# State space mixer of a two-layer backbone: running sums of log decays spread over partitions by way of DRAM, decayed products into one bank

## The chip, the core and the metric

The kernel runs on one core of a Trainium2 chip. The metric is the time of one execution on the device in microseconds (us). The engines are named as in the profile: PE (TensorE; PEld are its weight loads), DVE (VectorE), ACT (ScalarE), POOL (GpSimd) and SP (SyncE, which issues most DMAs). All arithmetic is float32; GEMM operands are split into a high and a low part of type fp32r.

## What is computed

Two layers of a hybrid block on 256 latent and 256 context tokens: an input projection feeds a bidirectional state space mixer (16 heads of 64, 4 groups with 128 states, chunks of 128 tokens) and a differential attention; both are gated, merged and followed by a gated MLP with a convolution. The change lies in the mixer alone. For each direction (the backward one on flipped tokens) the reference computes

```python
a = (dt * a_head)...; a_cs = jnp.cumsum(a, axis=-1)
cb = jnp.einsum('bclgn,bcsgn->bgcls', cc, bc)
decay_in = jnp.exp(segsum(a))            # exp(a_cs[l] - a_cs[s]) for s <= l, else 0
y_diag = jnp.einsum('bgcls,bgrcls,bcsgrp->bclgrp', cb, decay_in, xd)
...
y_off = jnp.einsum('bclgn,bcgrpn,bgrcl->bclgrp', cc, h_in, jnp.exp(a_cs))
y = (y_diag + y_off).reshape(bsz, n, n_heads, p)
```

## The kernel before

Channels lie on partitions, tokens on the free axis. In layer 0 four blocks t of 128 tokens are worked on (0 and 1 latent, 2 and 3 context, N = 512), in layer 1 the outputs of the two latent blocks alone (N = 256). Every GEMM goes through `gemm_f` (lines 379 to 413): SP loads weight tiles of 128x4x256 into `raw` (line 305, three buffers), ACT casts them to `whi` (line 314), DVE subtracts for `wlo` (line 315), and PE runs three matmuls per block of 128 rows (lines 408 to 410 where 512 columns are taken, 394 to 396 otherwise).

Beside the GEMMs run two lanes of generators. `pump()` (line 341) is called every six GEMM matmuls of 512 columns, or every twelve of 256, and moves each lane by one `yield`. So the program order of everything else follows the GEMM, and matmuls made by `pmm` keep that order on PE. The scheduler orders the other engines ahead of time; on the chip each engine takes its instructions in the fixed order.

In the state space stage the GEMMs are the projections of the inner channels (`xs`), of two pairs of gates and of `z`. Lane 0 runs `states(g)` for the four groups (lines 896 to 937): it transposes `xs` and B, weighs `xs` on POOL (line 920) and carries the states `h`. Lane 1 runs `outputs(g)` (lines 939 to 1010). Per group and block t it does:

- `head(t)`: the product `cb` of B and C, masked for both directions into `cbm` (line 950); then four products `at` on POOL (line 955), a triangular mask times the high and low part (`aH`, `aL`) of the log decays of four heads, for each direction;
- `seg`: four matmuls of 512 columns with a strict triangle `sgt` (line 970), which make the differences of running sums for both directions in one bank, and their Exp to `E` on ACT (line 972);
- X: for each head `cbm` times the step sizes of both directions (ACT line 976, DVE line 977), times E (line 978);
- `yoff`: C times the incoming state of each direction (line 988), each times `ecs`, the Exp of the running sums (DVE line 991, from PSUM), added up if there are two (line 995);
- `yd`: four products of `xT` and X with 64 columns of weights each (line 1000), then `yt` added to the same banks by a product with the identity (line 1003).

Blocks 0 and 1 have an incoming state from both directions, blocks 2 and 3 from one. At the end of a group `xs` takes `yd` and the skip term (line 1007), and the `z` GEMM's part waits for groups that are done (line 1033). The running sums and step sizes are made earlier, between the attention heads and the B projection (lines 817 to 858).

The profile names the PSUM banks by tag and use: `pmmmm` and `psmm` are GEMM banks, `psseg`, `psyoff`, `pscb`, `psstate`, `psssT` the banks of the lanes, `pyyd` the output bank. Lines of `pmm` and `ptr` are shown as L85 and L88.

## Time and profile before

| | |
|---|---|
| median of 3 runs | 1767.27 us (1766.97 to 1767.33) |
| the profiled execution, its own time | 1765.24 us |
| its span, first to last instruction | 1763.5 us |
| granted TensorE clock, mean | 0.995 |
| busy: PE, PEld, DVE, ACT, POOL | 96%, 81%, 66%, 47%, 12% |

"Busy" is the share of the span in which an engine had an instruction running. PE's matmuls are pipelined, so a PE that is busy need not be at its peak. Times inside the run count from the first instruction. In a list of groups the number behind the bar is the idle time ahead of the group's instructions and what ended it. Rows quoted from the trace stand in a section of their own below.

### The profile page before, as it was taken

The page shows a single profiled execution, that of the slowest core. Times are in us where ns is not written, and L with a number is a line of the kernel's source. Part 1 is how long each engine was busy: PE and PEld are TensorE (multiplying, and loading weights), DVE is VectorE, ACT ScalarE, POOL GpSimd, SP SyncE. Part 2 cuts the span into 40 slices and gives each one's busy share as a digit, 9 for nine tenths or more (in the row PEclk, how much of TensorE's full clock was granted, in tenths as well). Part 3 has the DMA queues.
Part 4 walks back from the last instruction along what each step waited for, and adds up shares of the span by engine and source line. Part 5 has one row for each costly group of instructions (what it writes and reads, how often), then busy time and mean ns, then how long its engine had stood idle before and what let it go on. Part 6 is the DMA issues. An engine that isn't in the chain of part 4 may idle for free. (4 is left out here: it accounts for less than half of the span.)

```text
span 1763.5 us, 26823 instructions
## 1 busy us (share of the span) xinstructions
PE 1697.9 (96%) x10483; PEld 1431.3 (81%) x10483; DVE 1159.8 (66%) x2017; ACT 830.3 (47%) x1545; POOL 220.0 (12%) x244
## 2 busy tenths in 40 slices
PE   6999999999998999999999999999999998989997
PEld 4788878777776788888888889788889787989997
DVE  4676677335679865666666326666675788769964
ACT  3565575323333433644444225556554443556653
POOL 3000000003356300300000002100001244010000
PEclk9999999999999999999999999999999999989999
DMA  9643433543220134232233335845435232556653
GB/s 316 205 134 120 128 113 110 178 156 121 59 72 26 51 103 139 89 94 89 93 95 93 96 105 159 251 145 155 146 94 177 75 90 78 179 168 186 187 180 118
DMA packets 226159, 227.98 MB, mean 129 GB/s; under 512 B 10269, under 2 KB 222656, under 8 KB 226032
## 3 DMA queue, kind: packets, MB, share of 16 engines
q1 hardware_dynamic: 224192, 224.56, 41.6%
...
HBM read 222.04 MB, written 4.19 MB: 128 GB/s over the span
## 5 line engine op out<-in xcount | busy, mean ns | idle before, releaser
L315 DVE TENSOR_TENSOR wlo<-raw,whi 128x1024 fp32r<-128x1024 f32 (+1 forms) x318 | 390.5, 1228 | 264.1 <-ACT whi L314 263.4
L314 ACT CAST whi<-raw 128x1024 fp32r<-128x1024 f32 (+1 forms) x318 | 329.4, 1036 | 400.2 <-PE pmmmm L409 164.3
L408 PE MATMUL pmmmm<-th,whi 128*128 128x512 f32 x744 | 307.2, 413 | 0.4 <-DVE chv L573 0.4
L409 PE MATMUL pmmmm<-tl,whi 128*128 128x512 f32 x744 | 295.6, 397 | 0.0
L410 PE MATMUL pmmmm<-th,wlo 128*128 128x512 f32 x744 | 295.0, 396 | 0.0
L408 PEld LDWEIGHTS pmmmm<-th,whi 128*128 128x128 f32 x744 | 140.0, 188 | 39.7 <-issue 7.5
L410 PEld LDWEIGHTS pmmmm<-th,wlo 128*128 128x128 f32 x744 | 139.8, 188 | 33.7 <-issue 1.0
L409 PEld LDWEIGHTS pmmmm<-tl,whi 128*128 128x128 f32 x744 | 140.2, 188 | 29.8 <-issue 1.4
L394 PE MATMUL pmmmm<-th,whi 128*128 128x256 f32 x480 | 139.2, 290 | 0.2 <-ACT th L543 0.2
L396 PE MATMUL pmmmm<-th,wlo 128*128 128x256 f32 x480 | 135.8, 283 | 0.8 <-DVE wlo L315 0.8
L395 PE MATMUL pmmmm<-tl,whi 128*128 128x256 f32 x480 | 135.5, 282 | 0.0
L394 PEld LDWEIGHTS pmmmm<-th,whi 128*128 128x128 f32 x480 | 91.3, 190 | 4.8 <-issue 3.6
L522 POOL TENSOR_TENSOR rs<-ms,mhalf 128x2 f32<-128x2 f32 x9 | 6.3, 699 | 692.3 <-DVE ms L519 692.3
L396 PEld LDWEIGHTS pmmmm<-th,wlo 128*128 128x128 f32 x480 | 91.1, 190 | 1.5 <-DVE wlo L315 1.4
L395 PEld LDWEIGHTS pmmmm<-tl,whi 128*128 128x128 f32 x480 | 91.4, 190 | 0.8 <-issue 0.4
L955 POOL TENSOR_TENSOR at<-kt,aH 128x512 fp32r<-128x512 f32 x48 | 58.0, 1208 | 182.0 <-PE pmmmm L410 100.5
L410 PE MATMUL psmm<-th,wlo 128*128 128x512 f32 x200 | 79.4, 397 | 0.0
L408 PE MATMUL psmm<-th,whi 128*128 128x512 f32 x200 | 79.1, 396 | 0.0
L409 PE MATMUL psmm<-tl,whi 128*128 128x512 f32 x200 | 79.1, 395 | 0.0
L728 ACT ACTIVATE e<-psscore,nmx 128x512 f32<-128x512 f32 (+1 forms) x96 | 58.1, 610 | 42.8 <-DVE nmx L725 39.9
L442 PE MATMUL pmmmm<-whi,th 128*128 128x256 f32 x256 | 74.4, 290 | 0.0
L725 DVE TENSOR_REDUCE nmx<-psscore 128x1 f32<-128x512 f32 (+1 forms) x80 | 51.9, 685 | 33.9 <-PE psscore L85 33.6
...
## 6 DMA issues: line engine op xcount, KB each, us to landing
raw<-in_w_in_dram SPq DMA_DIRECT2D x124, 512.0 KB, 4.0
raw<-in_w_up_dram SPq DMA_DIRECT2D x88, 512.0 KB, 3.5
mraw<-in_w_mod_dram SPq DMA_DIRECT2D x80, 512.0 KB, 4.6
raw<-in_w_down_dram SPq DMA_DIRECT2D x45, 512.0 KB, 3.6
boot<-in_w_mod_dram SPq DMA_DIRECT2D x16, 512.0 KB, 9.4
raw<-in_w_br_att_dram SPq DMA_DIRECT2D x16, 512.0 KB, 3.5
raw<-in_w_br_ssd_dram SPq DMA_DIRECT2D x16, 512.0 KB, 3.6
raw<-in_w_out_dram SPq DMA_DIRECT2D x16, 512.0 KB, 3.6
```

The costliest lines, as they stand in the source:

```text
L314: pin(A.copy(hi[:, 0:n, :], raw[:, 0:n, :]))
L315: pin(V.tensor_tensor(lo[:, 0:n, :], raw[:, 0:n, :], hi[:, 0:n, :].bitcast(F32), op=ALU.subtract))
L394: T.matmul(o[f], whi[:, kk, cs], xh, start=first, stop=False)
L395: T.matmul(o[f], whi[:, kk, cs], xl, start=False, stop=False)
L396: T.matmul(o[f], wlo[:, kk, cs], xh, start=False, stop=last)
L408: T.matmul(o, whi[:, k % 4, cs], hi[k][:, 0:n], start=k == 0, stop=False)
L409: T.matmul(o, whi[:, k % 4, cs], lo[k][:, 0:n], start=False, stop=False)
L410: T.matmul(o, wlo[:, k % 4, cs], hi[k][:, 0:n], start=False, stop=k == k_tiles - 1)
L442: T.matmul(b[:, n, :], hi[k][:, ts], whi[:, k % 4, :], start=k == 0 and n == 0, stop=False)
L725: V.tensor_reduce(nmx[:, cc, 0:ng], sc[cc].rearrange("p (g k) -> p g k", g=ng), axis=AX.X, op=ALU.max, negate=True)
L728: A.activation(e[cc][:, g * w:(g + 1) * w], sc[cc][:, g * w:(g + 1) * w], AF.Exp, bias=nmx[:, cc, g:g + 1], accum_out=sm[:, cc, g:g + 1])
L955: G.tensor_tensor(at, tri[dr].unsqueeze(1).to_broadcast([P, 4, P]), part.bitcast(F32)[:, t, 16 * dr + 4 * g:16 * dr + 4 * g + 4].unsqueeze ...
```

## The change

The differences of running sums are no longer made by matmuls. Once per layer, with the step sizes, four matmuls with the log decays as weights and both triangles as moving operand give the running sums with heads on partitions (`p3`); ACT copies them out, and POOL writes them to DRAM (`csd`) in 8 DMAs. `csc` keeps the running sums with tokens on partitions, as before, but without the Exp. For each block SP fetches four heads of both directions back as `cs`, each row repeated on all 128 partitions (0.5 MB, two buffers). From `cs` come

- `cc`: Exp of `cs` on ACT for the directions that the block has, times C on DVE, 128x1024 elements or 128x512;
- `E`: `cs` less `csc` on POOL, one subtraction of 128x512 per direction, in place; the minimum of both directions on DVE; Exp on ACT. The minimum picks the direction that the mask of `cbm` keeps.

The states then multiply `cc` straight into `yd`: per direction four products with 64 columns of weights each. `seg`, `yoff`, `yt` and the identity product are gone, and with them `sgt`, `aH`, `aL` and `ecs`. The fetch of block t+2 is issued behind X of block t; a block now takes three yields instead of six.

```diff
@@ -655,9 +653,8 @@
         BF = [mp.tile([P, 512], F32, name=f"BF{i}_{j}") for j in range(4)]
         CF = [mp.tile([P, N], F32, name=f"CF{i}_{j}") for j in range(4)]
         dtT = mp.tile([P, 4, 64], F32, name=f"dtT{i}")
-        aH = mp.tile([P, 4, 32], F32R, name=f"aH{i}")
-        aL = mp.tile([P, 4, 32], F32R, name=f"aL{i}")
-        ecs = mp.tile([P, 4, 32], F32, name=f"ecs{i}")
+        csc = mp.tile([P, 4, 32], F32, name=f"csc{i}")
+        csd = dp.tile([4, 2, 16, P], F32, name=f"csd{i}")
         ddt = mp.tile([P, 4, 32], F32, name=f"ddt{i}")
         etot = mp.tile([P, 4, 32], F32, name=f"etot{i}")
 
@@ -843,8 +840,6 @@
             V.scalar_tensor_tensor(dtT[:, :, 0:32], u, 0.0, lw, op0=ALU.max, op1=ALU.add)
             V.tensor_tensor(dtT[:, :, 32:64], dtT[:, :, 0:32], L["A"].unsqueeze(1).to_broadcast([P, 4, 32]), op=ALU.mult)
             av = dtT[:, :, 32:64]
-            V.tensor_copy(aH, av)
-            V.tensor_tensor(aL, av, aH.bitcast(F32), op=ALU.subtract)
             p1, p2 = bank("s"), bank("s")
             for n, lhs in enumerate((tri[0], tri[1], strict[0], strict[1])):
                 T.matmul(p1[:, n * P:(n + 1) * P], lhs, av, start=True, stop=True)
@@ -852,8 +847,18 @@
             p1v = p1.rearrange("p (n t c) -> p n t c", n=4, t=4)
             for dr in range(2):
                 cs = slice(16 * dr, 16 * dr + 16)
-                A.activation(ecs[:, :, cs], p1v[:, dr, :, cs], AF.Exp)
+                V.tensor_copy(csc[:, :, cs], p1v[:, dr, :, cs])
                 A.activation(ddt[:, :, cs], p1v[:, 2 + dr, :, cs], AF.Exp)
+
+            p3 = bank("s")
+            for t in range(4):
+                T.matmul(p3[32 * t:32 * t + 32, 0:256], av[:, t, :], kt[:, C_LE:C_LE + 256], start=True, stop=True)
+            csr = lp.tile([P, 256], F32, tag="h", name=nm("csr"), bufs=4)
+            A.copy(csr, p3[:, 0:256])
+            for t in range(4):
+                for dr in range(2):
+                    r = 32 * t + 16 * dr
+                    G.dma_start(csd[t, dr], csr[r:r + 16, dr * P:(dr + 1) * P])
             A.activation(etot, p2[:, 0:P].rearrange("p (t c) -> p t c", t=4), AF.Exp)
             V.tensor_tensor(ddt, ddt, dtT[:, :, 0:32], op=ALU.mult)
 
@@ -942,34 +947,44 @@
             xT, h_in = sh["xT"], sh["h"]
             yb = [bank("y", "yd"), bank("y", "yd")]
 
-            def head(t):
+            def fetch(t):
+                cs = up.tile([P, 2, 4, P], F32, tag="cs", name=nm("cs"), bufs=2)
+                nc.sync.dma_start(cs.rearrange("p d h l -> p d (h l)"),
+                                  csd[t, :, 4 * g:4 * g + 4, :].rearrange("d h l -> d (h l)").partition_broadcast(P))
+                return cs
+
+            def head(t, cs):
                 tsl = slice(t * P, (t + 1) * P)
                 cb = bank("s", "cb")
                 pmm(cb[:, 0:P], BF[g][:, tsl], CF[g][:, tsl], start=True, stop=True)
                 cbm = up.tile([P, 2, P], F32, tag="cbm", name=nm("cbm"), bufs=2)
                 V.tensor_tensor(cbm, cb[:, 0:P].unsqueeze(1).to_broadcast([P, 2, P]), tri2, op=ALU.mult)
-                ats = []
+
+                cc = up.tile([P, 2, 4, P], F32, tag="cc", name=nm("cc"), bufs=2)
+                dirs = [dr for dr in range(2) if not (dr == 0 and t == 2) and not (dr == 1 and t == 3)]
+                d0, d1 = dirs[0], dirs[-1] + 1
+                A.activation(cc[:, d0:d1], cs[:, d0:d1], AF.Exp)
+
                 for dr in range(2):
-                    for part in (aH, aL):
-                        at = up.tile([P, 4, P], F32R, tag="at", name=nm("at"), bufs=4)
-                        G.tensor_tensor(at, tri[dr].unsqueeze(1).to_broadcast([P, 4, P]),
-                                        part.bitcast(F32)[:, t, 16 * dr + 4 * g:16 * dr + 4 * g + 4].unsqueeze(2).to_broadcast([P, 4, P]),
-                                        op=ALU.mult)
-                        ats.append((dr, at))
-                return cbm, ats
-
-            nxt = head(0)
+                    G.tensor_tensor(cs[:, dr], cs[:, dr],
+                                    csc[:, t, 16 * dr + 4 * g:16 * dr + 4 * g + 4].unsqueeze(2).to_broadcast([P, 4, P]),
+                                    op=ALU.subtract)
+                V.tensor_tensor(cs[:, 0], cs[:, 0], cs[:, 1], op=ALU.min)
+                E = cs[:, 1]
+                A.activation(E, cs[:, 0], AF.Exp)
+                V.tensor_tensor(cc[:, d0:d1].rearrange("p d h l -> p (d h) l"), cc[:, d0:d1].rearrange("p d h l -> p (d h) l"),
+                                CF[g][:, tsl].unsqueeze(1).to_broadcast([P, 4 * (d1 - d0), P]), op=ALU.mult)
+                return cbm, cc, E, dirs
+
+            raw = fetch(0)
+            yield 1
+            nxt = head(0, raw)
+            if NT > 1:
+                raw = fetch(1)
             yield 1
             for t in range(NT):
                 tsl = slice(t * P, (t + 1) * P)
-                cbm, ats = nxt
-                yield 1
-
-                sg = bank("s", "seg")
-                for n, (dr, at) in enumerate(ats):
-                    pmm(sg, sgt[:, dr, :], at.rearrange("p h l -> p (h l)"), start=n == 0, stop=n == 3)
-                E = up.tile([P, 4, P], F32, tag="E", name=nm("E"), bufs=1)
-                A.activation(E, sg.rearrange("p (h l) -> p h l", h=4), AF.Exp)
+                cbm, cc, E, dirs = nxt
                 X = up.tile([P, 4, P], F32, tag="X", name=nm("X"), bufs=2)
                 for h in range(4):
                     dcol = [dtT[:, t, 16 * dr + 4 * g + h:16 * dr + 4 * g + h + 1] for dr in range(2)]
@@ -978,29 +993,21 @@
                 V.tensor_tensor(X, X, E, op=ALU.mult)
                 yield 1
                 if t + 1 < NT:
-                    nxt = head(t + 1)
+                    nxt = head(t + 1, raw)
                     yield 1
+                if t + 2 < NT:
+                    raw = fetch(t + 2)
                 while "done" not in sh:
                     yield None
-                dirs = [dr for dr in range(2) if (dr, t) in h_in]
-                yo = bank("s", "yoff")
-                for dr in dirs:
-                    pmm(yo[:, dr * 256:(dr + 1) * 256], CF[g][:, tsl], h_in[dr, t], start=True, stop=True)
-                yt = up.tile([P, 2, 4, 64], F32, tag="yt", name=nm("yt"), bufs=2)
-                for dr in dirs:
-                    V.tensor_tensor(yt[:, dr], yo[:, dr * 256:(dr + 1) * 256].rearrange("p (h q) -> p h q", h=4),
-                                    ecs[:, t, 16 * dr + 4 * g:16 * dr + 4 * g + 4].unsqueeze(2).to_broadcast([P, 4, 64]),
-                                    op=ALU.mult)
-                if len(dirs) == 2:
-                    V.tensor_tensor(yt[:, 0], yt[:, 0], yt[:, 1], op=ALU.add)
-                yield 1
-                ytv = yt[:, dirs[0]].rearrange("p h q -> p (h q)")
-                for h in range(4):
-                    r = slice(64 * (h % 2), 64 * (h % 2) + 64)
-                    pmm(yb[h // 2][r, tsl], xT[:, t, h * 64:(h + 1) * 64], X[:, h, :], start=True, stop=False)
-                yield 1
                 for f in range(2):
-                    pmm(yb[f][:, tsl], ytv[:, f * P:(f + 1) * P], ident, start=False, stop=True)
+                    for h in (2 * f, 2 * f + 1):
+                        r = slice(64 * (h % 2), 64 * (h % 2) + 64)
+                        pmm(yb[f][r, tsl], xT[:, t, h * 64:(h + 1) * 64], X[:, h, :], start=True, stop=False)
+                    for dr in dirs:
+                        for h in (2 * f, 2 * f + 1):
+                            r = slice(64 * (h % 2), 64 * (h % 2) + 64)
+                            pmm(yb[f][r, tsl], h_in[dr, t][:, h * 64:(h + 1) * 64], cc[:, dr, h, :],
+                                start=False, stop=dr == dirs[-1])
                 yield 1
             for f in range(2):
                 j = 2 * g + f
```

Left out of the diff: `sgt` and the copy into it. Behind the change all lines are a few higher: line 978 is 993 there, 930 is 935, 950 is 961, 315 is 314, 1007 is 1014; the fetch is 952, the subtraction 969, the minimum 972, the product for `cc` 975.

What the change does to the order on PE, seen where a block with one direction is finished in layer 0. Before, from the last `seg` matmul of the block to the product with the identity:

```order
2240 L85 MATMUL psseg_5256<-at_5244,sgt 128x512
2241 L85 MATMUL psyoff_5273<-h_4679,CF_2_621 128x256
2242 L85 MATMUL pscb_5301<-CF_3_622,BF_3_618 128x128
2243 L408 MATMUL pmmmm_5292<-th_253,whi_4872 128x512
2244 L409 MATMUL pmmmm_5292<-tl_254,whi_4872 128x512
2245 L410 MATMUL pmmmm_5292<-th_253,wlo_4873 128x512
2246 L408 MATMUL pmmmm_5292<-th_255,whi_5090 128x512
2247 L409 MATMUL pmmmm_5292<-tl_256,whi_5090 128x512
2248 L85 MATMUL pyyd_4998<-X_5263,xT_4604 64x128 x2
2249 L85 MATMUL pyyd_4999<-X_5263,xT_4604 64x128 x2
2250 L85 MATMUL pyyd_4998<-kt,yt_5275 128x128
2251 L85 MATMUL pyyd_4999<-kt,yt_5275 128x128
```

And now such a block (the same block t = 3 of the same group):

```order
2125 L407 MATMUL pmmmm_5039<-th_260,whi_5029 128x512
2126 L85 MATMUL pyyd_4788<-X_5067,xT_4566 64x128 x2
2127 L85 MATMUL pyyd_4788<-cc_5010,h_4643 64x128 x2
2128 L85 MATMUL pyyd_4789<-X_5067,xT_4566 64x128 x2
2129 L85 MATMUL pyyd_4789<-cc_5010,h_4643 64x128 x2
2130 L408 MATMUL pmmmm_5039<-tl_261,whi_5029 128x512
2131 L409 MATMUL pmmmm_5039<-th_260,wlo_5030 128x512
2132 L85 MATMUL psstate_5099<-xd_5083,bT_4939 128x256
```

All of a block's products now stand in one run between GEMM matmuls, and nothing of it is left ahead of them but `cb`. Behind the stage's first transposition 418 GEMM matmuls stood ahead of the last write into `yd` in layer 0, now 389; in layer 1 454, now 446.

On DVE in layer 0, before, from the product with E of one block into the work on its `yt`:

```order
593 L978 TENSOR_TENSOR X_5046<-X_5046,E_5044 128x512
594 L950 TENSOR_TENSOR cbm_5068<-pscb_5066,kt 128x256
595 L315 TENSOR_TENSOR wlo_5097<-raw_5088,whi_5096 128x1024
596 L1032 SCALAR_TENSOR_TENSOR zt_5078<-zt_5078,pmmmm_4984 128x512
597 L977 SCALAR_TENSOR_TENSOR X_5163<-cbm_5068,dtT_623,X_5163 128x128
598 L1034 TENSOR_TENSOR xs_3_3867<-xs_3_3867,zt_5078 128x512
599 L991 TENSOR_TENSOR yt_5112<-psyoff_5109,ecs_626 128x256 x2
600 L512 TENSOR_TENSOR acc_4786<-acc_4786,sqh_5082 128x256
601 L512 TENSOR_TENSOR acc_4788<-acc_4788,sqh_5085 128x256
602 L995 TENSOR_TENSOR yt_5112<-yt_5112 128x256
603 L930 TENSOR_TENSOR h_5148<-h_5064,etot_628 128x256
```

And now, where group 2 begins; the first row reads the last `cs` of group 1 and so releases the buffer for `cs_4814`, whose product for `cc` is row 575:

```order
568 L993 TENSOR_TENSOR X_4739<-X_4739,cs_4645 128x512
569 L975 TENSOR_TENSOR cc_4807<-cc_4807,CF_2_619 128x1024
570 L938 TENSOR_TENSOR h_4736<-h_4736,psstate_4734 128x256
571 L972 TENSOR_TENSOR cs_4790<-cs_4790 128x512
572 L935 TENSOR_TENSOR h_4800<-h_4736,etot_625 128x256
573 L1014 SCALAR_TENSOR_TENSOR xs_2_3876<-xs_2_3876,cols_157,pyyd_4490 128x512
574 L1014 SCALAR_TENSOR_TENSOR xs_3_3877<-xs_3_3877,cols_157,pyyd_4491 128x512
575 L975 TENSOR_TENSOR cc_4863<-cc_4863,CF_2_619 128x1024
576 L938 TENSOR_TENSOR h_4775<-h_4775,psstate_4773 128x256
577 L314 TENSOR_TENSOR wlo_4820<-raw_4666,whi_4819 128x1024
578 L935 TENSOR_TENSOR h_4856<-h_4775,etot_625 128x256
579 L972 TENSOR_TENSOR cs_4814<-cs_4814 128x512
```

The two products from PSUM and the addition have given way to a product on `cc` and a minimum, both with their inputs in SBUF, and six instructions stand between the release of a `cs` buffer and the first use of its next content.

## Rows read from the trace of the kernel before

**Rows 1.** Page of the whole run: busy us (share of the span) and instructions.
```profile
PE 1697.9 (96%) x10483; PEld 1431.3 (81%) x10483; DVE 1159.8 (66%) x2017; ACT 830.3 (47%) x1545; POOL 220.0 (12%) x244
```

**Rows 2.** Windows (first row: columns): state space stage of layer 0, its last third, layer 1's.
```profile
core 0: us, PE busy (x) PEld busy (x) DVE busy (x) ACT busy (x) POOL busy (x), PEclk, DMA share, GB/s
420.00:600.00 180.00, 168.26 (x869) 132.42 (x869) 147.04 (x242) 71.58 (x148) 89.81 (x84) 1.00 0.19 53
540.00:600.00 60.00, 51.77 (x278) 38.92 (x277) 55.84 (x94) 22.98 (x54) 35.09 (x32) 1.00 0.14 36
1400.00:1497.00 97.00, 90.42 (x616) 79.42 (x614) 82.09 (x143) 40.52 (x79) 43.41 (x42) 0.98 0.32 87
1450.00:1490.00 40.00, 34.59 (x246) 30.36 (x245) 38.94 (x75) 18.80 (x41) 20.58 (x19) 0.98 0.32 91
```

**Rows 3.** Timeline of PE in layer 0: start us, us, instruction, count, idle before.
```profile
539.00 1.18 PE L85 MATMUL psseg<-at,sgt 128*128 128x512 f32 x4
540.01 0.39 PE L408 MATMUL pmmmm<-th,whi 128*128 128x512 f32 x1
540.24 0.39 PE L409 MATMUL pmmmm<-tl,whi 128*128 128x512 f32 x1
...
543.46 1.02 PE L85 MATMUL psyoff<-h,CF 128*128 128x256 f32 x4
544.14 0.58 PE L408 MATMUL pmmmm<-th,whi 128*128 128x512 f32 x1
544.56 0.39 PE L409 MATMUL pmmmm<-tl,whi 128*128 128x512 f32 x1
...
546.28 0.66 PE L85 MATMUL pyyd<-X,xT 128*64 128x128 f32 x8
546.87 0.50 PE L408 MATMUL pmmmm<-th,whi 128*128 128x512 f32 x1
547.20 0.39 PE L409 MATMUL pmmmm<-tl,whi 128*128 128x512 f32 x1
...
551.28 0.71 PE L85 MATMUL pyyd<-kt,yt 128*128 128x128 f32 x4 [2.76 <-DVE yt L995]
551.75 0.48 PE L408 MATMUL pmmmm<-th,whi 128*128 128x512 f32 x1
```

**Rows 4.** Groups by line and form, DVE, 420 to 605 us: busy us, mean ns, idle before.
```profile
L977 DVE SCALAR_TENSOR_TENSOR X<-cbm,dtT,X 128x128 f32<-128x128 f32 x64 | 29.2, 501 | 2.4 <-ACT X L976 2.4
L315 DVE TENSOR_TENSOR wlo<-raw,whi 128x1024 fp32r<-128x1024 f32 x19 | 27.0, 1421 | 7.8 <-ACT whi L314 7.8
L978 DVE TENSOR_TENSOR X<-X,E 128x512 f32<-128x512 f32 x16 | 19.7, 1229 | 4.1 <-ACT E L972 4.1
L930 DVE TENSOR_TENSOR h<-h,etot 128x256 f32<-128x256 f32 x16 | 9.7, 609 | 0.1
...
L995 DVE TENSOR_TENSOR yt<-yt 128x256 f32<-128x256 f32 x8 | 5.1, 636 | 0.0
```

**Rows 5.** Single lines of DVE: shortest/median/longest ns, first and last start.
```profile
L977 DVE SCALAR_TENSOR_TENSOR X<-cbm,dtT,X x64: 333/342/1125, 426.7 to 594.9; 128x128 f32<-128x128 f32 x64
...
L315 DVE TENSOR_TENSOR wlo<-raw,whi x19: 1204/1226/2058, 419.8 to 600.9; 128x1024 fp32r<-128x1024 f32 x19
...
L978 DVE TENSOR_TENSOR X<-X,E x24: 675/1240/1529, 431.8 to 1493.7; 128x512 f32<-128x512 f32 x24
...
L991 DVE TENSOR_TENSOR yt<-psyoff,ecs x40: 405/410/425, 450.5 to 1494.7; 128x256 f32<-128x256 f32 x40
```

**Rows 6.** The same groups for POOL: busy us, mean ns of one.
```profile
L955 POOL TENSOR_TENSOR at<-kt,aH 128x512 fp32r<-128x512 f32 x30 | 36.8, 1227 | 32.5 <-PE psseg L85 32.4
```

**Rows 7.** DMA issues: engine, count, KB each, median us to landing.
```profile
raw<-in_w_in_dram SPq DMA_DIRECT2D x124, 512.0 KB, 4.0
...
fwb<-in_final_norm_w_dram POOLq DMA_DIRECT2D x1, 512.0 KB, 7.0
```

**Rows 8.** The same groups for ACT: busy us, mean ns of one.
```profile
L314 ACT CAST whi<-raw 128x1024 fp32r<-128x1024 f32 x18 | 18.8, 1046 | 22.1 <-PE pmmmm L409 22.1
```

2 lines of the change are left out of this document (removed).

## The prediction, made before the changed kernel ran

> **What bounds the kernel now.** I read the page first, then windows over the stretches that the change touches, then the groups of instructions and single lines in them.
>
> On the page PE is busy for 96% of the span [rows 1], so work taken off PE looks like time won. But the change lives in two stretches only: the state space stage of layer 0, roughly 420 to 600 us, and that of layer 1, 1400 to 1497 us. There the windows tell another story [rows 2]. In layer 0 PE is busy for 168.3 of 180 us and DVE for 147.0. In the last third of it DVE is busy for 55.8 of 60 us (0.93) while PE falls to 51.8. In layer 1 DVE has 82.1 of 97 us, and in the stretch 1450 to 1490 it has 38.9 of 40 (0.97) while PE has 34.6. So PE leads early in each stage and DVE late. What PE gives up is worth little once DVE is full, and the sum has to be made on DVE.
>
> DVE is also slower there than its work demands. A product of 128x512 takes 0.675 us at its shortest and 1.240 in the median, the 128x128 step on X between 0.333 and 1.125, and the weight split of 128x1024 between 1.204 and 2.058 [rows 5]. The multiplication of `yt`, of the same kind but reading PSUM, never leaves 0.405 to 0.425 [rows 5]. POOL is busy for 89.8 of those 180 us [rows 2]. I read the long ones as DVE and POOL in each other's way on SBUF.
>
> **What the change does to PE.** One step is one block t of one group g: 16 in layer 0, of which 8 have both directions and 8 have one, and 8 in layer 1, all with both. I price a run of matmuls from its start to the next GEMM matmul, plus the delay it leaves (GEMM matmuls otherwise follow each other every 0.23 us). `seg` takes 1.01 us. `yoff` with both directions takes 0.68, plus 0.42 less 0.23, which is 0.87. The eight 64-column instructions of X take 0.59 plus 0.33 less 0.23, which is 0.69. The identity product takes 0.47 [rows 3]. Removed are 1.01 + 0.87 + 0.47 = 2.35 with both directions, and 1.92 with one (half of `yoff`). Added are 16 or 8 more 64-column instructions. At 0.074 to 0.086 each (0.59/8, 0.69/8) 16 cost 1.18 to 1.38; I take 1.28, because the run gets longer, and 0.64 for 8. PE gains 1.07 or 1.28 a step: 18.8 us in layer 0, 8.6 in layer 1, 27.4 together.
>
> **What it does to DVE.** Layer 0 first. Removed: 24 products on `yoff` at 0.410 [rows 5] and 8 additions at 0.636 [rows 4], 14.9 us. Added, at undisturbed prices [rows 5]: 16 minima of 128x512 at 0.675, 8 products `cc` of 128x1024 at 1.226 and 8 of 128x512 at 0.675, 26.0 us.
>
> Then the disturbance. Above their undisturbed prices DVE paid 64 x (0.501 - 0.342) = 10.2, 16 x (1.229 - 0.675) = 8.9, 16 x (0.609 - 0.405) = 3.3 and 19 x (1.421 - 1.226) = 3.7, in all 26.1 us [rows 4, 5] (for L930 the undisturbed price is that of the same shape on L991). POOL loses 32 of its 64 `at` products at 1.227 us [rows 6], 39.3 of its 89.8 us, so 0.56 of the disturbance stays and 11.5 us go. The added instructions pay it too: the first three excesses make 22.4 on 39.2 undisturbed, 0.57, and 0.56 of that is 0.32, so 26.0 becomes 34.3. Net: 34.3 - 14.9 - 11.5 = +7.9 us.
>
> The Trainium skill (GPSIMD Engine Reference, section 1, Specifications) says that POOL's SBUF interface is shared with VectorE and that DVE instructions with two SBUF inputs contend for it. It speaks against this change: the removed product reads PSUM, the added ones read SBUF twice. Rows 5 agree for both kinds. What it would make of the sum is a rival below.
>
> Layer 1 by the same prices: 16 x 0.410 and 8 x 0.636 go (11.7), 8 x 0.675 and 8 x 1.226 come (15.2, disturbed 20.1), and half the relief, 5.7, goes. Net +2.7 us.
>
> **What is moved.** By the order of PE, 418 GEMM matmuls stood between the first transposition of the stage and the last write into `yd` in layer 0, now 389. The 29 that run later cost 29 x 0.23 = 6.7 us behind the stage and take 1.2 weight splits with them (1.7 us of DVE). Layer 1 goes from 454 to 446, which I leave out.
>
> **Where the end falls.** DVE's work is now 147.0 + 7.9 - 1.7 = 153.2 us and 82.1 + 2.7 = 84.8 us; PE's is 149.5 and 81.8. They are close, so neither runs undisturbed; DVE is the longer, and the time is its work over the share it is kept busy. That share was 0.82 and 0.85 over the stages, and 0.93 and 0.97 where DVE led [rows 2]. I take 0.91: nearer to the stretches where it led, since it now leads throughout, and a little under them, because its queue gains a wait for a DMA. Layer 0: 153.2/0.91 + 6.7 = 175.1, against 180: -4.9. Layer 1: 84.8/0.91 = 93.2, against 97: -3.8.
>
> **The smaller edits.** Four transposed running sums and one copy per layer come in the attention stage, where PE leads: 8 instructions of 256 columns between 0.06 and 0.22 each, 0.5 to 1.8 us per layer. I take 0.5 each, as the four write different partitions like the 64-column runs: +1. Two casts go and two copies come on DVE; two small Exp go from ACT. Both are nothing, and the copy of `sgt` ahead of the loop too. POOL issues 8 DMAs per layer, ahead of a head's `rs`; its owners wait several steps for that anyway. They land long before the stage, a whole attention merge earlier; without that cover one landing per layer would show.
>
> The 24 fetches move 24 x 0.5 MB, on DMA engines that are 0.19 and 0.32 busy [rows 2]: nothing by bandwidth. SP now stands behind X of the block two before, and the weight loads stand behind SP; but these wait for DVE too, for the split of an older tile, in the same order, so I count nothing. Without that cover a weight tile would come one landing late, 4.0 us [rows 7]. ACT gains an Exp of 128x1024 (about 1.05, as the cast of that shape [rows 8]) or half of it a step; at 71.6 busy of 180 it has room.
>
> **Sum.** -4.9 - 3.8 + 1 = -7.7. The profiled run took 1765.2, so 1757.5; the median of the runs is 2.0 above the profiled one, so 1759.6, rounded to **1760 us**. Zero is reached where DVE's share is 238.0/269.3 = 0.884. A measurement here tells about 0.2%, 3.5 us, from no change: faster needs a share over 0.895, slower one under 0.872.
>
> **Rivals.**
>
> *Both engines run full.* With fewer hand-overs between PE and DVE (no `seg`, no `yoff`) DVE could hold the 0.97 of layer 1's late stretch. 238.0/0.97 + 7.7 is 253.1 against 277, -23.9: 1743. For it: that stretch exists. Against: it is 40 us long, and PE would have to run 0.97 as well.
>
> *Nothing measurable.* A share of 0.88: 270.5 + 7.7 = 278.2, +1: 1768. For it: 0.88 lies between the two pairs of shares that the windows show.
>
> *Slower: the round trip of `cs`.* Each block has to wait for X two blocks before, then for the landing, Exp, two subtractions on POOL, the minimum and Exp again. In the second order of DVE shown above, the product on `cc` for the second block stands six instructions, about 5 us by [rows 4, 5], behind the release of its buffer. A landing of 4.0 and an Exp of 1.05 just fit. The only broadcast of that size in the trace, from POOL's queue, took 7.0 [rows 7]. Each microsecond beyond the fit empties DVE for up to 24 x 1 us, so landings of 5 us give -7.7 + 24 = +16: 1784. It decides from 0.32 us a block on (7.7/24). Against it: most places in the order have more than 5 us between release and use, and `fwb` went by another queue.
>
> *Slower: the added work meets POOL every time.* The added instructions then cost their disturbed prices, 1.240 for 24 of 128x512 in layer 0 (against 0.891 counted) and 2.058 for 8 of 128x1024 (against 1.618), and 8 of each in layer 1: 8.4 + 3.5 + 6.3 = 18.2, over 0.91 20.0. -7.7 + 20.0 = +12.3: 1780. Against: POOL is busy only about 0.3 of the time now (50.5 of 175 us), and its subtractions come before these instructions, not beside them. This is what the rule of the GPSIMD page comes to where it always bites.
>
> *The change does less than it says.* Outside the two stages and the running sums the orders of all five engines keep their sequence, so I give that no chance of its own.
>
> **Chances.** The forecast 0.42, both full 0.12, nothing 0.18, the round trip 0.20, POOL every time 0.08. Faster by over 0.2%: 0.54; within: 0.18; slower: 0.28. The range runs from 1744, near "both full", to 1781, past "POOL every time" and short of the worst round trip; about 0.1 is left out on either side. Of cases of both signs the forecast's own range is 1754 to 1764 (shares of 0.93 to 0.896).
>
> **What would show it.** PE's busy time falls by about 27 us in the two stages while DVE's rises by some 10; POOL's falls by about 60. The minimum and the 128x512 products should show medians under 1.0 us. If DVE sits idle before `cc` or before the minimum with ACT, POOL or a DMA as releaser for more than 8 us in all, the round trip was too long and the forecast is wrong. If PE is busy over 0.97 in both stages, I undervalued the gain.

## The result: 21 us faster, three times the forecast

The changed kernel takes 1746.12 us (median of 1740.01 to 1747.98) against 1767.12 before: ratio 0.9874, 95% interval 0.9856 to 0.9893, about 22 us less. That lies inside the range (1744 to 1781) and on the right side, but the forecast was 1760. The profiled execution of after is its fastest, 1740.01 us with a span of 1738.2; against 1765.24 before it shows 25 us less, and the rows below explain those 25. (Runs taken at other times are compared by their ratio to the kernel before, measured beside them; "us" of an experiment is (ratio - 1) x 1767.)

The page of after, busy time by engine, which answers to [rows 1]:

```profile
PE 1667.1 (96%) x10547; PEld 1406.2 (81%) x10547; DVE 1148.0 (66%) x2008; ACT 848.2 (49%) x1567; POOL 181.3 (10%) x212
```

PE lost 30.8 us (27 were forecast). DVE, which was to gain about 10, lost 11.8. POOL lost 38.7 instead of some 60: a subtraction took 1.45 us in the mean, and the 16 DMA issues count as 7.8 us of busy time. So PE's term was right and DVE's has the wrong sign.

To see where the time went, I count the weight casts on ACT, whose order and number (318) are the same in both kernels, and compare the times at which the same cast starts. The shift is -0.6 us shortly before the state space stage of layer 0, -14.5 behind it, -14.9 when that of layer 1, -25.2 behind it. So 13.9 us come from the one stage and 10.4 from the other; between them the shift wanders by up to 1.4 us and comes back. The windows below run from the 49th to the 73rd cast and from the 213th to the 249th, the same stretch of GEMM work in every kernel. First before (columns as in [rows 2]):

```profile
393.85:613.26 219.41, 207.11 (x1072) 161.78 (x1072) 166.11 (x276) 84.86 (x169) 96.22 (x90) 1.00 0.23 68
1361.36:1546.22 184.86, 175.70 (x1177) 156.11 (x1176) 147.04 (x252) 81.19 (x146) 58.03 (x58) 0.99 0.39 112
```

and after:

```profile
393.23:598.77 205.54, 187.89 (x1088) 146.24 (x1088) 160.84 (x278) 95.81 (x186) 61.71 (x58) 0.98 0.42 113
1346.50:1520.46 173.96, 162.55 (x1201) 146.00 (x1200) 142.10 (x244) 88.39 (x154) 45.67 (x42) 0.99 0.50 143
```

DVE fell by 5.3 and 4.9 us (forecast +7.9 and +2.7), although 24 minima and 24 products came and only 40 products on `yoff` with 16 additions went. PE fell by 19.2 and 13.2. And neither engine is full: in layer 0 PE has 0.91 of the stretch and DVE 0.78.

Where DVE's work went is in its groups over the first stretch, after (columns as in [rows 4]):

```profile
L314 DVE TENSOR_TENSOR wlo<-raw,whi 128x1024 fp32r<-128x1024 f32 x23 | 29.1, 1264 | 6.0 <-ACT whi L313 6.0
L992 DVE SCALAR_TENSOR_TENSOR X<-cbm,dtT,X 128x128 f32<-128x128 f32 x64 | 23.6, 415 | 1.2 <-ACT X L991 1.2
L972 DVE TENSOR_TENSOR cs<-cs 128x512 f32<-128x512 f32 x16 | 13.0, 811 | 7.8 <-POOL cs L969 7.8
L993 DVE TENSOR_TENSOR X<-X,cs 128x512 f32<-128x512 f32 x16 | 12.1, 755 | 0.2
L975 DVE TENSOR_TENSOR cc<-cc,CF 128x1024 f32<-128x1024 f32 x8 | 10.6, 1321 | 2.6 <-ACT cc L966 2.5
L935 DVE TENSOR_TENSOR h<-h,etot 128x256 f32<-128x256 f32 x16 | 7.5, 468 | 0.3 <-ACT h L933 0.3
L975 DVE TENSOR_TENSOR cc<-cc,CF 128x512 f32<-128x512 f32 x8 | 7.3, 914 | 5.6 <-ACT cc L966 5.6
L511 DVE TENSOR_TENSOR acc<-acc,sqh 128x256 f32<-128x256 f32 x14 | 7.2, 556 | 2.6 <-ACT sqh L510 2.6
L961 DVE TENSOR_TENSOR cbm<-pscb,kt 128x256 f32<-128x256 f32 x16 | 6.7, 416 | 0.1
...
L666 DVE SCALAR_TENSOR_TENSOR xs<-cth,chv 128x512 f32<-128x512 f32 x8 | 6.2, 772 | 1.8 <-ACT cth L665 1.5
...
L1041 DVE TENSOR_TENSOR xs<-xs,zt 128x512 f32<-128x512 f32 x8 | 5.5, 686 | 0.1
```

Three groups of the kernel before in the same stretch, which I had left out of the sum:

```profile
L512 DVE TENSOR_TENSOR acc<-acc,sqh 128x256 f32<-128x256 f32 x14 | 8.2, 625 | 1.0 <-ACT sqh L511 1.0
L669 DVE SCALAR_TENSOR_TENSOR xs<-cth,chv 128x512 f32<-128x512 f32 x8 | 7.1, 883 | 3.9 <-ACT cth L668 3.9
...
L1034 DVE TENSOR_TENSOR xs<-xs,zt 128x512 f32<-128x512 f32 x8 | 6.6, 824 | 0.1
```

The product with X fell from 1229 ns [rows 4] to 755, the step on X from 501 to 415, the state's product from 609 to 468. Instructions that both kernels have, unchanged, became 21 us cheaper in this stretch. `cbm`, which reads PSUM, stayed at 416 in both.

The reason can be watched in the kernel before. POOL from 570 us on (start us, us, instruction, idle before it):

```profile
571.91 1.04 POOL L955 TENSOR_TENSOR at<-kt,aH 128x512 fp32r<-128x512 f32 x1 [1.71 <-PE psseg L85]
572.91 1.49 POOL L955 TENSOR_TENSOR at<-kt,aL 128x512 fp32r<-128x512 f32 x1
574.36 1.08 POOL L955 TENSOR_TENSOR at<-kt,aH 128x512 fp32r<-128x512 f32 x1
575.41 1.08 POOL L955 TENSOR_TENSOR at<-kt,aL 128x512 fp32r<-128x512 f32 x1
```

and DVE meanwhile:

```profile
573.42 2.17 DVE L977 SCALAR_TENSOR_TENSOR X<-cbm,dtT,X 128x128 f32<-128x128 f32 x2
575.51 1.59 DVE L512 TENSOR_TENSOR acc<-acc,sqh 128x256 f32<-128x256 f32 x2
577.03 0.60 DVE L977 SCALAR_TENSOR_TENSOR X<-cbm,dtT,X 128x128 f32<-128x128 f32 x2
577.56 0.41 DVE L950 TENSOR_TENSOR cbm<-pscb,kt 128x256 f32<-128x256 f32 x1
577.89 0.68 DVE L978 TENSOR_TENSOR X<-X,E 128x512 f32<-128x512 f32 x1
```

While POOL works, two steps on X take 2.17 us; once it has stopped, at 576.5, two take 0.60, and the product with X its undisturbed 0.68. The Trainium skill (SBUF — State Buffer, "SBUF: two separate sides") says that POOL and a DVE instruction with two SBUF inputs exclude each other for a whole instruction. These rows agree: beside products of 1.04 to 1.49 us, DVE gets through about one instruction per product.

### The profile page after: what moved, and what is told of

Same layout as the page of the kernel before. It is cut to its first block, busy times and chain, and to the rows that moved or that the text cites. A ratio compares the mean times of both kernels' runs of the same rounds, so it can differ in the third digit from the quotient of the medians.

```text
span 1738.2 us, 27022 instructions
## 1 busy us (share of the span) xinstructions
PE 1667.1 (96%) x10547; PEld 1406.2 (81%) x10547; DVE 1148.0 (66%) x2008; ACT 848.2 (49%) x1567; POOL 181.3 (10%) x212
## 3 DMA queue, kind: packets, MB, share of 16 engines
q0 software_dynamic: 1312, 1.03, 0.2%
## 5 line engine op out<-in xcount | busy, mean ns | idle before, releaser
L969 POOL TENSOR_TENSOR cs<-cs,csc 128x512 f32<-128x512 f32 x48 | 69.1, 1454 | 264.0 <-DMA cs<-csd 141.5
L722 DVE TENSOR_REDUCE nmx<-psscore 128x1 f32<-128x512 f32 (+1 forms) x80 | 51.8, 684 | 34.3 <-PE psscore L85 34.2
```

The source lines that it names most:

```text
L722: V.tensor_reduce(nmx[:, cc, 0:ng], sc[cc].rearrange("p (g k) -> p g k", g=ng), axis=AX.X, op=ALU.max, negate=True)
L969: G.tensor_tensor(cs[:, dr], cs[:, dr], csc[:, t, 16 * dr + 4 * g:16 * dr + 4 * g + 4].unsqueeze(2).to_broadcast([P, 4, P]), op=ALU.subtract)
```

## The experiments

Theory D says that the stage is held up by DVE's work, which POOL's products lengthen; theory P that PE's work sets it; theory R that the round trip of the fetched sums does. Each diff is against after or before, as said. Sums over both stretches are compared: DVE 313.2 us before, 302.9 after; POOL 154.3 and 107.4.

**1. After, with POOL's products put back at a free place.**

```diff
+                for dr in range(2):
+                    at = up.tile([P, 4, P], F32, tag="at", name=nm("at"), bufs=2)
+                    G.tensor_tensor(at, tri[dr].unsqueeze(1).to_broadcast([P, 4, P]),
+                                    csc[:, t, 16 * dr + 4 * g:16 * dr + 4 * g + 4].unsqueeze(2).to_broadcast([P, 4, P]),
+                                    op=ALU.mult)
                 V.tensor_tensor(cs[:, 0], cs[:, 0], cs[:, 1], op=ALU.min)
```

> The changed kernel with two more POOL products of 128x512 per block (the kind that the change removed), written to a tile that nobody reads, right behind the two subtractions; the order of the other four engines stays as it is. POOL's busy time should rise by 48 products of about 1.2 us, some 58 us. Theory D (the stage is as long as DVE's work, and POOL's products lengthen DVE's): the minimum and the product with X go back over 1.0 us, DVE rises by 10 to 20 us, and the time by as much over 0.91: 1757 to 1768. Theory P (PE's work and its own waits set the stage, DVE has slack): DVE gets slower just the same, but the time stays within 4 us of the changed kernel, 1742 to 1750. If neither DVE nor the time changes, POOL's products disturb DVE less than I read from the trace of before.

Measured 1777.56 us, ratio 1.0042 (1.0023 to 1.0061), +7 us: more than any theory gave. But the added products depend on nothing in the block, and POOL ran nearly all of layer 0's ahead of the first subtraction:

```profile
409.54 30.41 POOL L974 TENSOR_TENSOR at<-kt,csc 128x512 f32<-128x512 f32 x27 [100.53 <-PE pmmmm L409]
439.90 4.04 POOL L969 TENSOR_TENSOR cs<-cs,csc 128x512 f32<-128x512 f32 x4
```

So the stage started late: by the cast's count layer 0 lost 25 us against after. It prices a blocked queue, not the contention; run 5 mends it. While POOL's instructions followed each other without a gap, a minimum on DVE took 7.50 us; it ended at 449.47, behind the last of them (448.92):

```profile
441.97 7.50 DVE L977 TENSOR_TENSOR cs<-cs 128x512 f32<-128x512 f32 x1 [17.91 <-POOL cs L969]
```

**2. After, with more work for PE alone.**

```diff
-                pmm(cb[:, 0:P], BF[g][:, tsl], CF[g][:, tsl], start=True, stop=True)
+                for n in range(5):
+                    pmm(cb[:, 0:P], BF[g][:, tsl], CF[g][:, tsl], start=True, stop=True)
```

> The changed kernel with the product into cb made five times instead of once in every block: four more 128x128 products, 96 in all, of about 0.14 us to the next start and 0.09 of delay behind, so 14 to 22 us of work for PE, nothing for the others. Theory P: the time rises by nearly all of it, 12 to 22 us, to 1758 to 1768. Theory D: PE has slack beside DVE, and the time rises by less than 7 us, to under 1753.

Measured 1756.33, ratio 0.9930 (0.9907 to 0.9952): 10 us over after, between the theories. PE's busy time rose by 22.9 us in the two stretches, so a microsecond of it costs 0.43.

**3. After, with more work for DVE alone.**

```diff
-                V.tensor_tensor(cbm, cb[:, 0:P].unsqueeze(1).to_broadcast([P, 2, P]), tri2, op=ALU.mult)
+                for n in range(3):
+                    V.tensor_tensor(cbm, cb[:, 0:P].unsqueeze(1).to_broadcast([P, 2, P]), tri2, op=ALU.mult)
```

> The changed kernel with the masking product from cb to cbm made three times in every block: 48 more products of 128x256 at 0.414 us (one input in PSUM, so little disturbed), 20 us of work for DVE, nothing for the others. Theory D: the time rises by 20/0.91, 22 us, to 1768. Theory P: by less than 7 us, to under 1753. In between: both engines hold each other up, and each microsecond of DVE's work has a price of its own, which is this run's quotient.

Measured 1754.42, ratio 0.9920 (0.9896 to 0.9944): 8 us over after. DVE's busy time rose by 13.9 us, so one microsecond of it costs 0.59. Neither theory is right alone: both engines hold each other up. These prices are rough: the intervals alone leave 0.2 to 0.7 for PE and 0.2 to 1.0 for DVE, the trace of after, from which the busy times are taken, is 6 us faster than its median, and the scheduler moved other instructions of DVE in both kernels.

**4. Before, with POOL's half alone.**

```diff
-                    for part in (aH, aL):
+                    for part in (aH,):
...
-                        ats.append((dr, at))
+                        ats.extend([(dr, at)] * 2)
```

> The kernel before, but POOL makes only the products of the high parts, and PE uses each of them twice: the same four products into seg, the same orders on DVE, ACT and SP, and half of POOL's at products (48 of 96). It leaves out the low part of the log decays (the high one counts twice). It is the relief that the change gives POOL, and nothing else. Theory D: DVE's excess of 26 us in layer 0 falls by more than half, DVE by 15 to 25 us in both stages together, and the time by 14 to 25 us: 1742 to 1753. Theory P: DVE falls as much, and the time by less than 4 us: 1763 to 1767. My prediction's own number, relief in proportion, is 11.5 + 5.7 = 17 us of DVE.

Measured 1748.83, ratio 0.9890 (0.9866 to 0.9914): -19 us, nearly the whole change, with not one instruction of PE or DVE altered. The windows:

```profile
393.56:604.43 210.87, 205.67 (x1072) 161.72 (x1072) 150.57 (x276) 85.13 (x168) 56.10 (x58) 1.00 0.24 71
1352.82:1527.61 174.79, 171.23 (x1162) 153.02 (x1161) 138.01 (x252) 81.22 (x146) 38.26 (x42) 1.00 0.40 118
```

The same number of DVE instructions took 15.5 and 9.0 us less, and PE's idle time went from 12.3 and 9.2 us to 5.2 and 3.6. Theory P falls. A microsecond of DVE was worth 19.4/24.6 = 0.8 here. The product with X did not gain; it still starts with POOL's remaining products:

```profile
L978 DVE TENSOR_TENSOR X<-X,E 128x512 f32<-128x512 f32 x16 | 19.8, 1236 | 4.1 <-ACT E L972 4.1
```

**5. After, with POOL's products put back beside DVE.**

The edit of run 1 with one line otherwise:

```diff
-                    G.tensor_tensor(at, tri[dr].unsqueeze(1).to_broadcast([P, 4, P]),
+                    G.tensor_tensor(at, cbm[:, dr, :].unsqueeze(1).to_broadcast([P, 4, P]),
```

> As the first of these runs, but the two added POOL products of a block read this block's cbm, so that they cannot run ahead of it: the order of POOL has them spread over the stage, behind the subtractions and beside DVE's steps on X, and the order of the other four engines is the changed kernel's. 48 products of about 1.2 us come on POOL, as many as the change removed. If POOL's products were what held DVE up in the kernel before (theory D), DVE's busy time rises by 12 to 20 us over the changed kernel in both stages and the time by 8 to 16 us, to 1754 to 1762. If the time stays under 1750, the relief of POOL is not what made the changed kernel fast, and the loss of the first run came from its 30 us of POOL products ahead of the stage alone.

Measured 1778.28, ratio 1.0046 (1.0029 to 1.0062): 30 us over after, and slower than before. Windows and groups of DVE:

```profile
394.35:621.72 227.37, 194.90 (x1088) 151.27 (x1088) 186.81 (x278) 95.84 (x186) 105.47 (x90) 0.95 0.38 102
1369.95:1554.50 184.55, 167.54 (x1199) 148.75 (x1198) 154.16 (x244) 88.10 (x155) 68.34 (x58) 0.96 0.48 134
```

```profile
L997 DVE SCALAR_TENSOR_TENSOR X<-cbm,dtT,X 128x128 f32<-128x128 f32 x64 | 34.9, 592 | 1.2 <-ACT X L996 1.2
...
L935 DVE TENSOR_TENSOR h<-h,etot 128x256 f32<-128x256 f32 x16 | 10.9, 679 | 0.3 <-ACT h L933 0.3
```

The orders of PE, DVE, ACT and SP are those of after, and nobody reads the added products, yet DVE rose by 38.0 us for 66.4 of POOL's time, and the time by 0.8 per microsecond of DVE. My range (12 to 20) was too small again: for each microsecond on POOL, DVE lost 0.57 here and 0.41 in run 4 (24.6 for 59.9), where I had counted 26.1/89.8 = 0.29.

POOL's longer queue could also have cost the time by itself, by coming late with what others wait for. But these waits did not grow: DVE waited 10.9 us for the subtractions in both stretches (13.4 in after), and PE 5.4 us (7.5 in after) for `xd`, POOL's weighing of `xs`. What grew is PE's wait for DVE's product with X. Layer 0, after and then run 5 (us, times, longest):

```profile
PE pyyd L85 <- DVE X L993: 8.2, 7, 2.1
PE psstate L85 <- POOL xd L925: 6.5, 4, 3.4
```

```profile
PE pyyd L85 <- DVE X L998: 22.4, 9, 5.9
PE psstate L85 <- POOL xd L925: 4.4, 3, 2.5
```

**6. After, with a tile of its own for the subtractions.**

```diff
+                sd = up.tile([P, 2, 4, P], F32, tag="sd", name=nm("sd"), bufs=1)
                 for dr in range(2):
-                    G.tensor_tensor(cs[:, dr], cs[:, dr],
+                    G.tensor_tensor(sd[:, dr], cs[:, dr],
...
-                V.tensor_tensor(cs[:, 0], cs[:, 0], cs[:, 1], op=ALU.min)
-                E = cs[:, 1]
-                A.activation(E, cs[:, 0], AF.Exp)
+                V.tensor_tensor(sd[:, 0], sd[:, 0], sd[:, 1], op=ALU.min)
+                E = sd[:, 1]
+                A.activation(E, sd[:, 0], AF.Exp)
```

> The changed kernel with a tile of its own for the two subtractions, the minimum and E, instead of working in the fetched tile: POOL needs no longer wait until ACT has read the sums for cc, and the next fetch can start once POOL and ACT have read the tile, not when X is done. Theory R (the round trip of cs holds the changed kernel up): ACT's waits for cs (12.4 and 9.4 us in the two stages) and DVE's for cc and for the subtractions (15.9 and 14.9) mostly go, and the time falls by 8 to 15 us, to 1731 to 1738. Theory D (work of PE and DVE): within 4 us of the changed kernel, 1742 to 1750.

Measured 1740.00, ratio 0.9841 (0.9816 to 0.9866): 6 us under after, between the two theories; the intervals just overlap. DVE's wait for `cc` went, but it now waited 18.7 us for POOL's subtractions in layer 0 (7.8 in after); in the whole run its waits for both rose from 30.7 to 36.2 us. Its work fell, though, by 11.2 us in the two stretches:

```profile
399.55:602.31 202.76, 187.21 (x1088) 146.41 (x1088) 154.36 (x278) 96.38 (x187) 63.20 (x58) 0.98 0.41 115
1350.98:1524.32 173.34, 163.07 (x1204) 146.53 (x1203) 137.42 (x244) 89.07 (x154) 40.34 (x42) 0.99 0.51 144
```

So the 6 us need not come from a shorter round trip: at 0.6 to 0.8 each, less work on DVE gives 7 to 9.

**7. Before, with half of `seg`.**

```diff
-                for n, (dr, at) in enumerate(ats):
-                    pmm(sg, sgt[:, dr, :], at.rearrange("p h l -> p (h l)"), start=n == 0, stop=n == 3)
+                for n, (dr, at) in enumerate(ats[0::2]):
+                    pmm(sg, sgt[:, dr, :], at.rearrange("p h l -> p (h l)"), start=n == 0, stop=n == 1)
```

> The kernel before, with POOL's four products as they are, but only the two of the high parts multiplied into seg: two matmuls of 128x512 less per block (48 in all, by the rows 0.23 us each and more with the delay behind, so 11 to 13 us less work for PE), the same POOL and DVE work. It leaves out the low part of the log decays. Theory D (DVE, held up by POOL, sets the end of the stage): less than 5 us are won, 1762 to 1768. Theory P (PE's work sets it): 8 to 13 us, 1754 to 1760.

Measured 1762.59, ratio 0.9965 (0.9953 to 0.9976): -6 us, between the theories, with 9.9 us less PE work. But it is no clean price of PE: DVE's work fell by 8.2 us too, with POOL's as before (157.4 us), and the mean of the product with X went from 1229 to 939 ns. The shorter `seg`, and the order that came with it, move POOL's products against DVE's work.

**8. After, with every fetch twice.**

```diff
-                nc.sync.dma_start(cs.rearrange("p d h l -> p d (h l)"),
-                                  csd[t, :, 4 * g:4 * g + 4, :].rearrange("d h l -> d (h l)").partition_broadcast(P))
+                for n in range(2):
+                    nc.sync.dma_start(cs.rearrange("p d h l -> p d (h l)"),
+                                      csd[t, :, 4 * g:4 * g + 4, :].rearrange("d h l -> d (h l)").partition_broadcast(P))
```

> The changed kernel with every fetch of cs issued twice into the same tile, the second behind the first: twice the bytes, and by the 5.7 us that a landing takes in the trace 6 us more until the sums can be read. Theory R: every block waits for it, and the time rises by more than 15 us, to over 1761, up to 24 x 6 = 144 us where nothing hides it. Theory D: the fetches are mostly early enough, and it rises by less than 8 us, to under 1754.

Measured 1783.37, ratio 1.0080 (1.0059 to 1.0101): 36 us over after. DVE did less work than in after (293.9 us in both stretches), so this is waiting, as theory R has it: ACT stood 35.8 us before its Exp for the sums in layer 0 (12.4 in after). The changed kernel has little slack in its round trip. A fetch lands after 5.7 us in the median (4.9 to 8.8), not the 4.0 of a weight tile [rows 7].

**9. The half of the change that makes E.** After, with the offsets as before: no `cc`, and the lines of `yoff`, `ecs`, `yt` and the identity product back.

```diff
-                A.activation(cc[:, d0:d1], cs[:, d0:d1], AF.Exp)
...
+                A.activation(ecs[:, :, cs], p1v[:, dr, :, cs], AF.Exp)
...
+                    pmm(yo[:, dr * 256:(dr + 1) * 256], CF[g][:, tsl], h_in[dr, t], start=True, stop=True)
...
+                    pmm(yb[f][:, tsl], ytv[:, f * P:(f + 1) * P], ident, start=False, stop=True)
```

> Half of the change: E comes from the running sums (fetch, two POOL subtractions, minimum, Exp; no at products, no seg), the offsets stay as in the kernel before (yoff, ecs, yt, the identity product). By the runs so far a microsecond of DVE's work is worth about 0.8 us and one of PE's about 0.5. PE loses seg, 24 x 1.01 = 24 us, DVE gains 24 minima, 16 to 20 us, and loses by POOL's relief what the changed kernel lost, 20 to 30 us. Theory D (prices of both, POOL's relief the larger part): -12 for PE and -3 to -8 for DVE, 1748 to 1754. Theory R (the round trip of cs costs more than E by seg): above 1760.

Measured 1762.32, ratio 0.9973 (0.9960 to 0.9986): only 5 us under before and in the range of theory R, though DVE's busy time fell by 20.7 us. DVE stood before the minimum; who waited for whom on DVE in layer 0 (us, times, longest):

```profile
DVE cs L969 <- POOL cs L966: 27.9, 10, 5.1
```

**10. The half that makes the offsets.** Before, with `at`, `seg` and E as they are, the sums fetched into `cc`, and the products of state and `cc` in place of `yoff`, `yt` and the identity.

```diff
+                A.activation(cc[:, d0:d1], cc[:, d0:d1], AF.Exp)
...
-                    pmm(yb[f][:, tsl], ytv[:, f * P:(f + 1) * P], ident, start=False, stop=True)
+                            pmm(yb[f][r, tsl], h_in[dr, t][:, h * 64:(h + 1) * 64], cc[:, dr, h, :],
+                                start=False, stop=dr == dirs[-1])
```

> The other half: E by at and seg as in the kernel before, with POOL's 96 products, and the offsets as in the changed kernel (sums fetched into the tile cc, Exp, product with C, straight to the output bank). PE's balance is near zero (removed 0.87 + 0.47 per block with both directions, added 1.28). DVE loses 26.6 us of yt and gains 25 us of products that read SBUF twice, beside twice as much POOL work. Theory D: no gain, or a loss by the disturbance of the added products: 1766 to 1780. If this half alone gains over 5 us (under 1762), the saving of yoff and the identity product is worth more than I count.

Measured 1785.06, ratio 1.0100 (1.0078 to 1.0122): 18 us over before, more than theory D gave. DVE's work is that of before (312.0 us in both stretches), but PE waited 17.3 us in layer 0 for the product with X, where it had waited 4.2. Which of the waits in front of that product cost it I did not separate. The halves together make +13, the whole change -22.

**11. Before, with half of `at` and half of `seg`.** The first line of run 4, and two matmuls as in run 7.

```diff
-                    for part in (aH, aL):
+                    for part in (aH,):
...
-                    pmm(sg, sgt[:, dr, :], at.rearrange("p h l -> p (h l)"), start=n == 0, stop=n == 3)
+                    pmm(sg, sgt[:, dr, :], at.rearrange("p h l -> p (h l)"), start=n == 0, stop=n == 1)
```

> The kernel before with the low parts left out for good: half of POOL's at products and half of the matmuls into seg. It leaves out the low part of the log decays. If the two savings add up as they came alone (-20 and -7 us), 1740 to 1744. Theory P': once DVE is relieved PE alone sets the end, and its 11 to 13 us come in full: 1735 to 1739. If DVE still sets it, the seg half adds less than 4 us: over 1746.

Measured 1739.58, ratio 0.9838 (0.9818 to 0.9859), -29 us: a little more than the sum of the two (-19 and -6). PE fills 0.97 of both stretches. Once DVE is relieved, PE's work is worth some 9 of its 11 to 13 us (the intervals leave 4 to 15).

**12. After, with the subtractions on ACT.**

```diff
-                V.tensor_copy(csc[:, :, cs], p1v[:, dr, :, cs])
+                V.tensor_scalar(csc[:, :, cs], p1v[:, dr, :, cs], -1.0, None, op0=ALU.mult)
...
-                    G.tensor_tensor(cs[:, dr], cs[:, dr],
-                                    csc[:, t, 16 * dr + 4 * g:16 * dr + 4 * g + 4].unsqueeze(2).to_broadcast([P, 4, P]),
-                                    op=ALU.subtract)
+                    for h in range(4):
+                        n = 16 * dr + 4 * g + h
+                        A.activation(cs[:, dr, h, :], cs[:, dr, h, :], AF.Identity, bias=csc[:, t, n:n + 1])
```

> The changed kernel with the two subtractions of a block on ACT, as eight additions of 128x128 with a column of the negated sums as bias (0.39 us each by ACT's steps on X, 3.1 us a block), and none on POOL, which keeps xd only. ACT has room on average (96 of 206 us), but it makes E's chain no shorter. Theory D: what is left of POOL's disturbance goes, DVE falls by 8 to 15 us in the two stages, the time by 6 to 12 us: 1734 to 1740. Theory R (the chain from the landing to E counts): two waits between engines go, ACT's queue gets 3.1 us longer; no gain or a loss, 1746 to 1760.

Measured **1722.83 us**, ratio 0.9744 (0.9725 to 0.9763): 45 us under before and 23 under after. This version leaves nothing out and is faster than both kernels. Windows and groups of DVE:

```profile
395.06:587.50 192.44, 183.88 (x1088) 143.99 (x1088) 148.16 (x278) 131.44 (x314) 19.12 (x26) 1.00 0.47 121
1336.21:1501.78 165.57, 160.10 (x1200) 144.54 (x1199) 136.42 (x244) 106.02 (x219) 20.30 (x26) 1.00 0.54 150
```

```profile
L992 DVE SCALAR_TENSOR_TENSOR X<-cbm,dtT,X 128x128 f32<-128x128 f32 x64 | 19.7, 357 | 1.1 <-ACT X L991 1.1
L972 DVE TENSOR_TENSOR cs<-cs 128x512 f32<-128x512 f32 x16 | 11.1, 696 | 2.4 <-ACT cs L971 2.2
L993 DVE TENSOR_TENSOR X<-X,cs 128x512 f32<-128x512 f32 x16 | 11.0, 686 | 0.2
```

Every group is back near its undisturbed price; DVE falls by 18.4 us, the time by 23, both more than theory D gave. At 0.6 to 0.8 each the work on DVE makes 11 to 15 of the 23. With POOL's subtractions went also DVE's waits for them (13.4 us in after, here 2.4 for ACT's) and PE's for `xd`, and the clock is 1.00 here; which of these made the rest I did not separate.

**13. Run 6, with one fetch per layer.**

```diff
-                                  csd[t, :, 4 * g:4 * g + 4, :].rearrange("d h l -> d (h l)").partition_broadcast(P))
...
+                                      csd[0, :, 0:4, :].rearrange("d h l -> d (h l)").partition_broadcast(P))
+                    once.append(cs)
+                return once[0]
...
```

> The kernel with a tile of its own for the subtractions (the sixth run, 1740), with one fetch per layer instead of sixteen or eight: every block reads the sums of the first block of the first group, and subtracts that block's column. The blocks' own decays are left out, the work on all engines is the same, and the order of PE and POOL is that of the sixth run. Theory R (the landing of cs still holds the blocks up): 6 to 15 us less than the sixth run, 1725 to 1734. Theory D (what is left is work, and POOL's subtractions beside DVE): within 4 us of it, 1736 to 1744.

Measured 1739.37, ratio 0.9821 (0.9799 to 0.9843), which the measurement can't tell from run 6. With a tile of its own the landing costs nothing more that shows. What the round trip costs in after stays open: run 6 is no price of it, as DVE's work fell there too.

**14. Run 9, with the subtractions on ACT,** by the lines of run 12.

> The first half of the change (E from the running sums, the ninth run, 1762) with the subtractions on ACT as in the twelfth. In the ninth DVE stood 28 us in layer 0 before the minimum, waiting for POOL's subtraction, with other work queued behind. If that wait ate the gain of the half, the time falls to 1738 to 1750. If the landing of cs did, which stays as it is, the time stays within 5 us, 1757 to 1767.

Measured 1752.15, ratio 0.9906 (0.9877 to 0.9935): 12 us under run 9 by the ratios and 2 us above the end of the range. The landing was left as it is, so the larger part of what run 9 lost was POOL's subtractions. Whether by DVE's wait for them or by the work they made on DVE, which fell by 15.0 us, this run does not tell.

**15. Before, with the products of the low parts on ACT.**

```diff
+                        if part is aH:
+                            G.tensor_tensor(at, tri[dr].unsqueeze(1).to_broadcast([P, 4, P]),
...
+                        else:
+                            for h in range(4):
+                                n = 16 * dr + 4 * g + h
+                                A.activation(at[:, h, :], tri[dr], AF.Copy, scale=part.bitcast(F32)[:, t, n:n + 1])
```

> The kernel before with only the products of the low parts moved to ACT, as activations of 128x128 with the decay as scale: eight per block at 0.39 us, 75 us in all, and POOL relieved of 48 of its 96 products. Nothing is left out, PE and DVE have the same work. Theory D: as the run with the high parts alone, 1747 to 1756, so that this alone would be worth about as much as the whole change. If ACT's 3.1 us per block stand in the way of X and E, 1758 or more.

Measured 1750.72, ratio 0.9894 (0.9877 to 0.9911): -19 us with all of the computation kept. Moving 48 products from POOL to ACT is alone worth about what the whole change is.

## Why the prediction was wrong in size

**What bounds the kernel: half right.** I read that PE leads early and DVE late, and then made the sum on DVE alone, work over a share of 0.91. The runs price a microsecond of DVE at 0.6 to 0.8 (runs 3, 4, 5) and one of PE at about 0.4 (run 2), or 0.7 to 0.9 once DVE is relieved (run 11). My formula had 1/0.91 = 1.1 and 0. The share itself was not met: DVE's 0.78 of layer 0's stretch in after is near the 0.76 of before. By the measured prices and my own terms, PE's -27.4 x 0.43 and DVE's +7.9 + 2.7 - 1.7 = +8.9 x 0.8 give -4.7, close to the -7.7 that I forecast. That is luck: the forecast gain came from a rising share, which did not rise, and PE's saving, which I had at nothing, is of the same size. So the formula, although wrong, was not what made the number wrong.

**PE's saving: right.** 27.4 us were forecast, 30.8 are on the page.

**DVE's disturbance: the step that failed.** I wrote that 0.56 of the disturbance stays and 11.5 us go, and that the added instructions pay a factor of 1.32. Between the two kernels the shared groups of the first stretch fell by 2.9 (weight split), 5.6 (steps on X), 7.6 (product with X), 2.2 (states) and 3.0 (the three groups that I hadn't counted): 21.3 us instead of 11.5. The added instructions took 30.9 instead of 34.3, the removed ones 14.4 instead of 14.9. Net -4.8 by these rows (-5.3 measured) instead of +7.9; in layer 1 -4.9 instead of +2.7. That is 21 us of DVE too much, and at 0.8 each 17 us of time: -4.7 becomes -21, and -22 was measured. The sum is no better than its prices: with PE at 0.7 it would be nearly -29. How the 22 us divide between PE's saving and DVE's relief is not shown more closely.

Two things made it too small. Relief is in proportion to POOL's work only where the order stays; otherwise it depends on what stands beside it. In layer 0 of run 4 the four groups of my sum fell by 9.9 of 26.1 us, 0.38, for 0.42 of POOL's time; in after by 18.3, 0.70, for 0.36. In the kernel before, `seg` reads the old `at` and so sets POOL free for the next ones just when E and the product with X come; that product cost 1229 ns. In after the subtractions are released by the landing and by ACT, and it costs 755. Run 4 kept POOL's release where it was and halved the work: 1236. And I counted only four groups: the others gave 3.0 us in after and some 6 in run 4.

**The rivals.** "Both engines run full" gave 1743 and so comes nearest, but not by its mechanism: DVE's share did not rise, its work fell. The round trip is real (DVE stood 30.7 us in the whole run before `cc` and the minimum, where I had set 8 as the mark, and run 8 shows how little slack there is). By my own sign it should have made the kernel slower than forecast, and it did not: what these waits cost is not priced (runs 6 and 13), but the relief outweighs it. That added work would meet POOL every time was wrong: the minimum has a median of 686 ns, the product with X 682:

```profile
L972 DVE TENSOR_TENSOR cs<-cs x16: 675/686/1518, 420.9 to 572.0; 128x512 f32<-128x512 f32 x16
L993 DVE TENSOR_TENSOR X<-X,cs x16: 674/682/1530, 433.6 to 574.8; 128x512 f32<-128x512 f32 x16
```

**The small edits** were small, as forecast: where the running sums are made, at 249 and 1273 us, the shift of the casts changes by 0.8 and 0.2 us (0.5 each was forecast), no more than it wanders where the kernels are alike.
